# A hybrid decoder layer: the first norm's residual made in quarters beside the recurrence, and one branch chunk's seven products moved from the first block to the third

## The chip, the core and the metric

The kernel runs on one core of a Trainium2 chip. It is one launch that computes one decoder layer for 256 tokens in float32. The metric is the time on the device in microseconds, the lower the better. A core has engines that each run their own queue of instructions in order: TensorE (PE; PEld is its weight load) for matrix products, VectorE (DVE) and ScalarE (ACT) for elementwise work, GpSimd (POOL) and SyncE (SP), which in this kernel mostly issue DMA transfers. Engines wait for each other through semaphores.

## The reference

What matters of it here: a first SwiGLU with a residual and a norm gives `h`; from `h` come attention, a gated recurrence and gates; both branches are merged, and the residual of `h` is added again.

```python
h = layer_norm(DN_ALPHA * h + 0.5 * swiglu(h, ffn1_w_in[l], ffn1_w_out[l]), ln1_g[l], ln1_b[l])
q, k, v, qi, ki, wi, rx, rg, gates = split_cols(h @ w_in[l])
...
y_attn = dsa_attention(q, k, v, qi, ki, wi)
y_rnn = rglru_branch(rx, rg, conv_w[l], conv_b[l], lru_wa[l], lru_ba[l],
                     lru_wx[l], lru_bx[l], lru_lambda[l])
g_attn, g_rnn = jnp.split(jax.nn.sigmoid(gates), 2, axis=-1)
merged = g_attn * (y_attn @ w_attn_branch[l]) + g_rnn * (y_rnn @ w_rnn_branch[l])
h = layer_norm(DN_ALPHA * h + merged @ w_out[l], ln2_g[l], ln2_b[l])
h = layer_norm(DN_ALPHA * h + 0.5 * swiglu(h, ffn2_w_in[l], ffn2_w_out[l]), ln3_g[l], ln3_b[l])
```

The model width is 2048, the recurrence 2560 wide, and the layer norm ends with a product by `g` and a sum with `b`.

## The kernel before

**Weights.** Every weight matrix streams from HBM through SBUF once, in pieces of up to 128x1024 (class `Weights`). A piece is loaded by SP into a `raw` buffer (five of them), then split for exact products: ACT writes the high part `wh` (L245) and DVE the low part `wl` (L246), each with five buffers. The piece's number stands in the names that the lists of instructions below show: `wl585` is the low part of piece 585, loaded into `raw585`. SP can load piece n+5 only when DVE has split piece n. Some stretches of 4 x 128 rows (a chunk) are multiplied by seven products of half size in place of eight; such a chunk is loaded whole into an `rf` buffer (three of them), and DVE makes sums of its blocks first (`operand`, L208, L212, L215). `YR_FAST` says for each of the four 512-column blocks of the recurrent branch's product which of its five chunks are made that way; the others are plain.

**Order.** PE, SP and POOL run in the order in which the program is written. The order of DVE and ACT is set by a scheduler when the kernel is built, by its own estimate of when each operand is there; on the chip it is fixed. Work that is to run beside the products is written as generators; `Background.step` advances each by one `yield` whenever PE starts on a new piece.

**The recurrence** (the loop over `NR + LAG`) takes 80 pieces of `wB` and 24 of `lru`, pieces 570 to 673. Two pieces make one product of a 128-column block (`block3`, `wide3`: for each 128 rows L1437 with the high part, 512 columns, and L1438 with the low part, 256 columns). DVE then reduces the result (L1456, tile `t`), applies three taps of a convolution (L1476, tile `xg`) and splits it (L832, tile `xc`). After it come two gate blocks (pieces 674 to 689) and the recurrent branch's product (from piece 690), whose matrix products L716, L717 and L719 are those of `together`.

**The residual.** `h` after the first norm is needed again after the merge. Its normalized rows lie in DRAM in eight tiles `away[t][nb]` (two of 128 tokens, four of 512 columns; `ys37` to `ys44` in the lists), put there without gain and bias. While the recurrence runs, `residual_away` borrows the three `rf` buffers (tile `ry`): it loads the gain row for all partitions and the eight tiles, multiplies on DVE (L677), adds the bias with a DMA that accumulates in SBUF (L679), and stores the result to the same DRAM tiles (L681). All its DMAs are issued by POOL. `back` (L687) loads them later. A similar routine for the second norm, `residual`, adds its bias by L660; L1132 accumulates the feed-forward's partial results.

Of the kernel before, what the change touches and what calls it, by code (L numbers as in the profile page):

```python
# [12 lines left out]
OP = mybir.AluOpType  # L13
# [4 lines left out]
D = 2048  # L18
# [51 lines left out]
def block_plan(chunks, fills, lead=2, n=4, late=True):  # L70

    plain = [("c", k) for q in range(n) if q not in chunks for k in (4 * q, 4 * q + 2)]
    forms = [(f, q) for q in chunks for f in FORMS]
    rest = ["o"] * fills
    plan = [(rest.pop(), 0) for _ in range(min(lead, fills))] + plain[:1]
    plain = plain[1:]
    slow = []
    while plain or rest:  # L80
        for which in (plain, rest) if late else (rest, plain):
            if which:
                p = which.pop(0)
                slow.append((p, 0) if p == "o" else p)
    if not forms:
        return plan + slow
    step = len(forms) / (len(slow) + 1)
    n = 0
    for i, f in enumerate(forms):
        plan.append(f)  # L90
        while len(slow) > n and i + 1 >= (n + 1) * step:
            plan.append(slow[n])
            n += 1
    return plan
# [13 lines left out]
A_FAST = {b: () if b == 6 else ONE_A if b in (5, 1) else FAST_A for b in range(8)}  # L108
GATE_FAST = ((), (), (), (3,), FAST_A, FAST_A, (), ())
YA_FAST = ((), (0, 1), (0, 1), (0, 1))  # L110
YR_FAST = ((0, 1), (0, 1), (0,), (0,))
MG_FAST = ((), (0, 1), (0,))
YA_FORMS = (0, 1)
YR_FORMS = (0, 1)
# [207 lines left out]
def tile_layer(ctx, tc, x_fm, x_tm, pos, f1a, f1o, wA, wki, wB, wG, lru, wab, wrb, wo, f2a, f2o,  # L322
# [6 lines left out]
    V, A, T, G = nc.vector, nc.scalar, nc.tensor, nc.gpsimd  # L329
    count = [0]  # L330

    def name(s):
        count[0] += 1
        return f"{s}{count[0]}"

    def U(s="u", dt=F32):
        return pool.tile([P, 512], dt, name=name(s), tag="u", bufs=U_BUFS)
# [4 lines left out]
    def T1(s="t"):  # L342
        return temps.tile([P, S], F32, name=name(s), tag="t", bufs=T_BUFS)
# [22 lines left out]
    def block_pieces(ap, plan, fills=None, fo=None):  # L366
        chunk = {}
        for f, k in plan:
            if f == "c":
                pieces.append((ap[:, k * 512:k * 512 + PIECE], None))  # L370
            elif f == "o":
                g, nb, k = next(fills)
                k += 2 * SEGS[g][0]
                pieces.append((fo[nb][:, k * 512:k * 512 + PIECE], None))
            else:
                if k not in chunk:
                    chunk[k] = ap[:, k * 2048:(k + 1) * 2048]
                pieces.append((chunk[k], f))
# [28 lines left out]
    for i in range(NR + LAG):  # L407
        if i < NR:
            plain([wB[RX + i], wB[RG + i]])
        if i >= LAG:  # L410
            g, c = divmod(i - LAG, TPG)
# [5 lines left out]
    for b in range(4):  # L417
        block_pieces(wrb[b], block_plan(YR_FAST[b], 0, 0, NR // 4))
    for nb in range(3):
# [227 lines left out]
    def bias_row(b, nb, w=512):  # L647
        return bass.AP(tensor=b.tensor, offset=b.offset + nb * 512, ap=[[0, P], [1, w]])
# [13 lines left out]
    def residual_away(g, b):  # L662

        def wide():
            return W.fast_pool.tile([P, D], F32, name=name("ry"), tag="rf", bufs=RAWF_BUFS)

        gr, ys = wide(), [wide() for _ in range(2)]
        G.dma_start(gr, bias_row(g, 0, D))
        for t in range(2):
            for nb in range(4):  # L670
                G.dma_start(ys[t][:, nb * 512:(nb + 1) * 512], away[t][nb])
        for _ in range(8):
            yield
        for t in range(2):
            for o in range(0, D, 512):
                v = ys[t][:, o:o + 512]
                V.tensor_tensor(v, v, gr[:, o:o + 512], op=OP.mult)  # L677
                yield
            G.dma_start(ys[t], bias_row(b, 0, D), accum_op=OP.add)  # L679
            for nb in range(4):  # L680
                G.dma_start(away[t][nb], ys[t][:, nb * 512:(nb + 1) * 512])  # L681

    def back():
        for nb in range(4):
            for t in range(2):
                Y[t][nb] = U("y")
                G.dma_start(Y[t][nb], away[t][nb])  # L687
            yield
# [458 lines left out]
    away = [[spill.tile([P, 512], F32, name=name("ys")) for _ in range(4)] for _ in range(2)]  # L1147
# [12 lines left out]
    qT, kT, v, qiT = [None] * 8, [None] * 2, [None] * 2, [None] * 4  # L1160
# [186 lines left out]
    def token_tiles():  # L1347
        return [[spill.tile([P, 512], F32, name=name("gd")) for _ in range(2)] for _ in range(4)]

    ga, gr = token_tiles(), token_tiles()  # L1350
# [3 lines left out]
    def product(x, forms, fast):  # L1354

        c, e = blockF(x, forms, block_plan(fast, 0, 0, len(x) // 4), None)
        return (joined(c, e), True) if e else (c, False)
# [9 lines left out]
    def fetch(src):  # L1367
        r = []
        for t in range(2):
            u = U("gf")  # L1370
            G.dma_start(u, src[t])
            r.append(u)
        return r
# [11 lines left out]
    for nb in range(4):  # L1385
        g, got = got, fetch(ga[nb + 1]) if nb < 3 else None
        s, _ = product(ya, ya_forms, YA_FAST[nb])
# [62 lines left out]
    def block3(x):  # L1450
# [6 lines left out]
        return t  # L1457

    bg.add("away", residual_away(ln1_g, ln1_b))
    xgs, xcs, tiles = {}, {}, []  # L1460

# [6 lines left out]
    for j in range(NR + LAG):  # L1468
# [14 lines left out]
        if j >= LAG:  # L1483
            i = j - LAG
            g, c = divmod(i, TPG)
# [7 lines left out]
            vw, t = U("vw"), T1()  # L1493
# [3 lines left out]
            if c == TPG - 1:  # L1497
# [6 lines left out]
                vw, t, u = U("vw"), T1(), T1()  # L1504
                for n in range(2):
                    a, b = slice(64 * n, 64 * n + 64), slice(64 - 64 * n, 128 - 64 * n)
# [34 lines left out]
    for nb in range(4):  # L1541
        if nb == 3:
            bg.add("main", back())
        s, _ = product(yr, yr_forms, YR_FAST[nb])
        g, a = got
# [18 lines left out]
def _layout(x, positions, ffn1_w_in, ffn1_w_out, ln1_g, ln1_b, w_in, conv_w, conv_b, lru_wa, lru_ba,  # L1564
# [4 lines left out]
    def c(a):  # L1569
        return np.ascontiguousarray(a)  # L1570
# [12 lines left out]
    def f_in(w, plans):  # L1583
        fast = [sorted({k for f, k in plan if f in FORMS}) for plan in plans]
        return paired(w.reshape(NK, P, 2, NBK, 256).transpose(3, 1, 0, 2, 4).reshape(NBK, P, NK, 512), fast)

    def f_out(w):
        return paired(w.reshape(NKF, P, 4, 512).transpose(2, 1, 0, 3), [()] * 4)

    def a_blocks(w, fast):  # L1590
        n = w.shape[1] // 512
        nk = w.shape[0] // P
        return paired(w.reshape(nk, P, n, 512).transpose(2, 1, 0, 3), fast)
# [13 lines left out]
    def recurrent(wa, wx):  # L1607
        lr = np.zeros((GRP, P, 16, P), wa.dtype)
        for g in range(GRP):
            for c in range(GRP):  # L1610
                a, x = wa[g * GRP + c], wx[g * GRP + c]
                row = slice(32 * c, 32 * c + 32)
                x_col = slice(32 * (c ^ 2), 32 * (c ^ 2) + 32)
                half = 10 + 3 * (c // 2)
                for n, m, col in ((0, a, row), (1, x, x_col)):
                    lr[g, row, n] = m[P:, :P]
                    lr[g, :, 2 * c + 2 + n] = m[:P, :P]
                    lr[g, :, half + c % 2, col] = m[:P, P:]
                    lr[g, row, half + 2, col] = m[P:, P:]
        return lr.reshape(GRP, P, -1)  # L1620
# [4 lines left out]
    def pr(vec):  # L1625
# [11 lines left out]
        lru=recurrent(lru_wa[0], lru_wx[0]), wab=a_blocks(w_attn_branch[0], YA_FAST),  # L1637
        wrb=a_blocks(w_rnn_branch[0][order], YR_FAST),
        wo=a_blocks(w_out[0], MG_FAST + ((),)), f2a=f_in(ffn2_w_in[0], PLANS2), f2o=f_out(ffn2_w_out[0]), cols_d=c(cols),
# [18 lines left out]
```

## Time and profile before

| | |
|---|---|
| Time, median of 3 runs | 2234.37 us (2232.87 to 2234.55) |
| The profiled execution: its time | 2234.3 us |
| The profiled execution: its span | 2232.5 us |
| ACT busy | 1423.6 us (64%) |
| Moved from HBM | 468.83 MB read, 12.58 MB written |
| Chain that ended last, by engine | PE 66%, issue 26%, DVE 3%, DMA 2%, POOL 2% |

The span runs from the first instruction to the last; the time has 1.8 us around it. In the rows of the profile, a group is a line of the program on one engine, with the tiles it writes and reads; "x8 | 5.4, 687" means eight instructions, 5.4 us in total, 687 ns each on average; what follows names the idle time of the engine just before them and what ended it. In a timeline each row begins with the start and the duration in microseconds. In a row of waits stand who waited, for whom, the sum, the number of waits and the longest. In a row of stretches of time (`1366.70:1392.30`) stand the length, then the busy time of PE, PEld, DVE, ACT and POOL, the granted PE clock as a share of full speed, the DMA engines' busy share and their GB/s. "DMA to landing" is the time from the issue of a transfer to its completion (least, median, greatest).

### The profile page before, as it was taken

Reading aid. Unit: us, or ns where it says so; the run is one execution under the profiler, and the core shown is the slowest. Engines: PE = TensorE matmul, PEld = TensorE weight load, DVE = VectorE, ACT = ScalarE, POOL = GpSimd, SP = SyncE. Lnnn points to the kernel's source line nnn. Section 1 sums busy time; section 2 is a strip of 40 time slices with the busy share of each in tenths; the row PEclk is TensorE's granted clock in tenths of the full one; section 3 lists DMA queues with packets and bytes.
Section 4 is the critical chain, followed back from the end, with each engine's and each line's share of the span. In section 5 each row is a group of like instructions: output and inputs, shape, how many; then the busy total and the mean of one; then the engine's idle time right before and its main releaser. Section 6 shows DMA issues by size and latency. Waiting matters only on the chain.

```text
span 2232.5 us, 37406 instructions
## 1 busy us (share of the span) xinstructions
PE 2218.2 (99%) x13942; PEld 2034.9 (91%) x13942; DVE 2113.9 (95%) x3076; ACT 1423.6 (64%) x1967; POOL 136.2 (6%) x210
## 2 busy tenths in 40 slices
PE   9999999999999999999999999999999999999998
PEld 8999999999998898899989988998899999999997
DVE  8999999999999999799979889999999999999997
ACT  6666666666656655665567786555666666666663
POOL 0000000000001000001100001100100000000001
PEclk9999999999999999999999999999999999999999
DMA  9776766666675555648686658765877667676655
GB/s 341 235 227 227 237 214 224 237 221 235 228 238 200 185 197 174 208 141 309 231 280 200 192 186 311 253 216 190 260 235 230 237 219 243 219 245 216 218 200 189
DMA packets 128086, 504.83 MB, mean 226 GB/s; under 512 B 14848, under 2 KB 17664, under 8 KB 108832
## 3 DMA queue, kind: packets, MB, share of 16 engines
q1 hardware_dynamic: 107424, 451.98, 57.8%
q0 software_dynamic: 20480, 50.46, 9.6%
q8 instruction: 109, 1.79, 0.3%
q14 instruction: 73, 0.60, 0.1%
HBM read 468.83 MB, written 12.58 MB: 216 GB/s over the span
## 4 chain that ended last, share of the span: by engine, by line
PE 66%; issue 26%; DVE 3%; DMA 2%; POOL 2%; ACT 1%; SPq 0%; DVEq 0%; POOLq 0%; ACTq 0%
PE mm L716 14%; PE mm L719 13%; PE mm L717 13%; PE mm L1437 6%; PE bp L719 4%; PE bp L717 4%; PE bp L716 4%; PE mm L1438 3%; POOL y L1132 1%; DVE wl L246 1%; PE mm L704 1%; PE mm L702 1%; PE mm L703 1%; ACT wh L245 1%; DMA rf<-f2a 0%
## 5 line engine op out<-in xcount | busy, mean ns | idle before, releaser
L245 ACT ACTIVATE wh<-raw 128x1024 fp32r<-128x1024 f32 (+1 forms) x569 | 572.5, 1026 | 264.0 <-PE mm L717 174.4
L246 DVE TENSOR_TENSOR wl<-raw,wh 128x1024 fp32r<-128x1024 f32 (+1 forms) x569 | 661.3, 1182 | 55.8 <-ACT wh L245 55.0
L245 ACT ACTIVATE wh<-rf 128x1024 fp32r<-128x1024 f32 (+1 forms) x438 | 393.3, 914 | 191.8 <-PE mm L717 105.2
L246 DVE TENSOR_TENSOR wl<-rf,wh 128x1024 fp32r<-128x1024 f32 (+1 forms) x438 | 450.5, 1041 | 6.6 <-PE mm L719 1.2
L716 PE MATMUL mm<-wh,hs 128*128 128x512 f32 (+1 forms) x872 | 297.3, 350 | 0.0
L717 PE MATMUL mm<-wh,hs 128*128 128x512 f32 (+1 forms) x872 | 292.1, 344 | 0.0
L716 PE MATMUL mm<-wh,g 128*128 128x512 f32 x656 | 249.3, 380 | 0.0
L717 PE MATMUL mm<-wh,g 128*128 128x512 f32 x656 | 248.6, 379 | 0.0
L245 ACT ACTIVATE wh<-ws 128x1024 fp32r<-128x1024 f32 x146 | 155.4, 1064 | 120.5 <-PE mm L717 72.2
L716 PE MATMUL bp<-wh,sh 128*128 128x256 f32 x876 | 213.6, 278 | 0.0
L1437 PE MATMUL mm<-hs,wh 128*128 128x512 f32 x640 | 211.4, 383 | 1.1 <-ACT wh L245 1.1
L717 PE MATMUL bp<-wh,sl 128*128 128x256 f32 x876 | 210.7, 275 | 0.0
L719 PE MATMUL mm<-wl,hs 128*128 128x512 f32 (+1 forms) x872 | 205.1, 344 | 0.0
L208 DVE TENSOR_TENSOR ws<-rf 128x1024 f32<-128x1024 f32 x146 | 178.2, 1220 | 11.0 <-DMA rf<-f2a 3.9
L246 DVE TENSOR_TENSOR wl<-ws,wh 128x1024 fp32r<-128x1024 f32 x146 | 177.9, 1218 | 3.9 <-ACT wh L245 3.7
L716 PEld LDWEIGHTS mm<-wh,hs 128*128 128x128 f32 x872 | 165.8, 190 | 15.3 <-issue 1.3
L717 PEld LDWEIGHTS mm<-wh,hs 128*128 128x128 f32 x872 | 165.9, 190 | 13.6
L1438 PE MATMUL mm<-hs,wl 128*128 128x256 f32 x640 | 175.0, 273 | 1.7 <-DVE wl L246 1.7
L717 PEld LDWEIGHTS bp<-wh,sl 128*128 128x128 f32 x876 | 168.1, 192 | 1.2
L716 PEld LDWEIGHTS bp<-wh,sh 128*128 128x128 f32 x876 | 168.0, 192 | 1.2
L719 PE MATMUL mm<-wl,g 128*128 128x512 f32 x656 | 168.3, 379 | 0.0
L719 PEld LDWEIGHTS mm<-wl,hs 128*128 128x128 f32 x872 | 153.8, 190 | 15.5
(374 smaller groups left out, 4616.9 us busy)
## 6 DMA issues: line engine op xcount, KB each, us to landing
rf<-f1a SPq DMA_DIRECT2D x57, 1024.0 KB, 6.1
rf<-f2a SPq DMA_DIRECT2D x57, 1024.0 KB, 6.2
raw<-f1o SPq DMA_DIRECT2D x88, 512.0 KB, 7.8
raw<-f2o SPq DMA_DIRECT2D x88, 512.0 KB, 7.8
raw<-wB SPq DMA_DIRECT2D x80, 512.0 KB, 4.5
raw<-f2a SPq DMA_DIRECT2D x62, 512.0 KB, 3.9
raw<-f1a SPq DMA_DIRECT2D x61, 512.0 KB, 3.8
raw<-wG SPq DMA_DIRECT2D x54, 512.0 KB, 3.8
```

What stands on the lines that cost most here:

```text
L208: v.tensor_tensor(t, b[:, 0:4:3], b[:, 1:2].to_broadcast([P, 2, 4, P]), op=OP.add)
L245: self.last_h = nc.scalar.activation(hp, src, AF.Copy)
L246: self.last = nc.vector.tensor_tensor(lp, src, hp, op=OP.subtract)
L702: T.matmul(ps, xh, w[0], start=start, stop=False)
L703: T.matmul(ps, xh, w[1], start=False, stop=False)
L704: T.matmul(ps, xl, w[0], start=False, stop=stop)
L716: T.matmul(ps, xh, w[0], start=start, stop=False)
L717: T.matmul(ps, xl, w[0], start=False, stop=False)
L719: T.matmul(ps, xh, w[1], start=False, stop=stop)
L1132: G.dma_start(Y[t][nb], u, accum_op=OP.add)
L1437: T.matmul(ps.rearrange("p (a q h) -> p a q h", a=2, h=2), w[0], both, start=first, stop=False)
L1438: T.matmul(ps[:, :S].rearrange("p (q h) -> p q h", h=2), w[1], pairs(x[:, 0]), start=False, stop=last)
```

## The change

```diff
-YR_FAST = ((0, 1), (0, 1), (0,), (0,))
+YR_FAST = ((0,), (0, 1), (0, 1), (0,))
...
         gr, ys = wide(), [wide() for _ in range(2)]
-        G.dma_start(gr, bias_row(g, 0, D))
-        for t in range(2):
-            for nb in range(4):
-                G.dma_start(ys[t][:, nb * 512:(nb + 1) * 512], away[t][nb])
-        for _ in range(8):
-            yield
-        for t in range(2):
-            for o in range(0, D, 512):
-                v = ys[t][:, o:o + 512]
-                V.tensor_tensor(v, v, gr[:, o:o + 512], op=OP.mult)
+        for nb in range(4):
+            part = [v[:, nb * 512:(nb + 1) * 512] for v in (gr, *ys)]
+            G.dma_start(part[0], bias_row(g, nb, 512))
+            yield
+            for t in range(2):
+                G.dma_start(part[1 + t], away[t][nb])
                 yield
-            G.dma_start(ys[t], bias_row(b, 0, D), accum_op=OP.add)
-            for nb in range(4):
-                G.dma_start(away[t][nb], ys[t][:, nb * 512:(nb + 1) * 512])
+            for _ in range(5):
+                yield
+            for t in range(2):
+                V.tensor_tensor(part[1 + t], part[1 + t], part[0], op=OP.mult)
+                yield
+                G.dma_start(part[1 + t], bias_row(b, nb), accum_op=OP.add)
+            for _ in range(8):
+                yield
+            for t in range(2):
+                G.dma_start(away[t][nb], part[1 + t])
+                yield
```

The residual is made in four quarters of 512 columns, one after the other, each with its own gain load, two loads of y, two products, two accumulations and two stores, all of 256 KB; before, the gain and each accumulation were 1 MB, and the loads came first, then the products, then accumulations and stores. The bytes are the same. The number of DMAs goes from 19 to 28. In the branch, the second chunk is made by seven products in the blocks 2 and 3, no longer in 1 and 2, and the host lays out the weights accordingly. Lines after the change stand four lower than before (L246 is still L246; L1456 becomes L1460).

POOL's queue at the residual, before: from the last load to the first store of the second half (`ry787` and `ry788` are the two y tiles, `ry786` the gain, `ln1_b` the bias).

```order
L671 DMA ry788_12086<-ys44_235 128x512
L679 DMA ry787_12085<-ln1_b 128x2048
L681 DMA ys37_228<-ry787_12085 128x512
L681 DMA ys38_229<-ry787_12085 128x512
L681 DMA ys39_230<-ry787_12085 128x512
L681 DMA ys40_231<-ry787_12085 128x512
L679 DMA ry788_12086<-ln1_b 128x2048
L681 DMA ys41_232<-ry788_12086 128x512
```

POOL's queue now, from the start of the first quarter to the loads of the second:

```order
L670 DMA ry786_12084<-ln1_g 128x512
L673 DMA ry787_12085<-ys37_228 128x512
L673 DMA ry788_12086<-ys41_232 128x512
L680 DMA ry787_12085<-ln1_b 128x512
L680 DMA ry788_12086<-ln1_b 128x512
L684 DMA ys37_228<-ry787_12085 128x512
L684 DMA ys41_232<-ry788_12086 128x512
L670 DMA ry786_12084<-ln1_g 128x512
L673 DMA ry787_12085<-ys38_229 128x512
L673 DMA ry788_12086<-ys42_233 128x512
```

The loads of a quarter now stand behind the stores of the quarter before it, and a store reads what the accumulation has written. No other DMA of POOL stands between the quarters: the next one in its queue belongs to the gate blocks after the recurrence.

DVE's queue in the recurrence, before, at the splits of pieces 582 to 585 (`wl`), with the last two residual products in it:

```order
L246 TENSOR_TENSOR wl582_12299<-raw582_12145,wh582_12298 128x256
L677 TENSOR_TENSOR ry788_12086<-ry788_12086,ry786_12084 128x512 x2
L246 TENSOR_TENSOR wl583_12322<-raw583_12167,wh583_12321 128x1024
L1456 TENSOR_REDUCE t801_12342<-mm800_12295 128x256
L246 TENSOR_TENSOR wl584_12356<-raw584_12193,wh584_12355 128x1024
L1476 SCALAR_TENSOR_TENSOR xg802_12344<-t801_12342,cols_120,xg802_12344 128x255
L1476 SCALAR_TENSOR_TENSOR xg802_12344<-t801_12342,cols_120,xg802_12344 128x254
L1476 SCALAR_TENSOR_TENSOR xg802_12344<-t801_12342,cols_120,xg802_12344 128x253
L246 TENSOR_TENSOR wl585_12379<-raw585_12215,wh585_12378 128x1024
```

DVE's queue now at the same place. `ry788` in it is the second product of the second quarter, `ry787` the first product of the third:

```order
L246 TENSOR_TENSOR wl582_12293<-raw582_12138,wh582_12292 128x256
L678 TENSOR_TENSOR ry788_12086<-ry788_12086,ry786_12084 128x512
L246 TENSOR_TENSOR wl583_12316<-raw583_12161,wh583_12315 128x1024
L1460 TENSOR_REDUCE t801_12337<-mm800_12289 128x256
L246 TENSOR_TENSOR wl584_12351<-raw584_12187,wh584_12350 128x1024
L1480 SCALAR_TENSOR_TENSOR xg802_12339<-t801_12337,cols_120,xg802_12339 128x255
L1480 SCALAR_TENSOR_TENSOR xg802_12339<-t801_12337,cols_120,xg802_12339 128x254
L1480 SCALAR_TENSOR_TENSOR xg802_12339<-t801_12337,cols_120,xg802_12339 128x253
L678 TENSOR_TENSOR ry787_12085<-ry787_12085,ry786_12084 128x512
L836 TENSOR_TENSOR xc803_12344<-xg802_12339,xc803_12344 128x256
L246 TENSOR_TENSOR wl585_12374<-raw585_12209,wh585_12373 128x1024
L678 TENSOR_TENSOR ry788_12086<-ry788_12086,ry786_12084 128x512
```

Before, all eight products are behind DVE at split 583. Now the third quarter's products stand on both sides of split 585. The first quarter's stand on both sides of split 578, the second's around a reduction and split 582, and the fourth's here, between splits 588 and 589:

```order
L246 TENSOR_TENSOR wl588_12456<-raw588_12290,wh588_12455 128x1024
L678 TENSOR_TENSOR ry787_12085<-ry787_12085,ry786_12084 128x512
L1460 TENSOR_REDUCE t811_12475<-mm810_12430 128x256
L678 TENSOR_TENSOR ry788_12086<-ry788_12086,ry786_12084 128x512
L246 TENSOR_TENSOR wl589_12489<-raw589_12313,wh589_12488 128x1024
L1480 SCALAR_TENSOR_TENSOR xg812_12477<-t811_12475,cols_120,xg812_12477 128x255
```

SP's queue at the start of the recurrent branch, before, with the whole-chunk loads `rf691` and `rf698`, and now, with `rf691` alone in the first block and `rf703` as the second block's first:

```order
L181 DMA raw690_14988<-wrb 128x1024
L181 DMA rf691_15008<-wrb 128x2048
L181 DMA raw693_15059<-wrb 128x1024
L181 DMA raw695_15111<-wrb 128x1024
L181 DMA raw697_15162<-wrb 128x1024
L181 DMA rf698_15194<-wrb 128x2048
```

```order
L181 DMA raw690_14997<-wrb 128x1024
L181 DMA rf691_15017<-wrb 128x2048
L181 DMA raw692_15046<-wrb 128x1024
L181 DMA raw693_15070<-wrb 128x1024
L181 DMA raw695_15122<-wrb 128x1024
L181 DMA raw696_15151<-wrb 128x1024
L181 DMA raw698_15205<-wrb 128x1024
L181 DMA raw699_15229<-wrb 128x1024
L181 DMA raw701_15303<-wrb 128x1024
L181 DMA raw702_15321<-wrb 128x1024
L181 DMA rf703_15339<-wrb 128x2048
```

The first block's second whole-chunk load has become two plain ones; the second block begins with piece 702 in place of 704.

## The prediction

> **What bounds the kernel now.** I read the page first, then the waits and busy times of the stage that the change touches (1095 to 1150 us, the start of the recurrence), then its timelines engine by engine, and last the times that single DMAs took to land.
>
> ```profile
> span 2232.5 us, 37406 instructions
> PE 2218.2 (99%) x13942; PEld 2034.9 (91%) x13942; DVE 2113.9 (95%) x3076; ACT 1423.6 (64%) x1967; POOL 136.2 (6%) x210
> ```
>
> TensorE (PE) is busy for 99% of the span, so a change that leaves its products alone can only win back the few places where PE waits, or make new ones. VectorE (DVE) has 95%: it has hardly any slack to hide a wait of its own. What PE waits for between 1095 and 1400 us:
>
> ```profile
> PE mm L1438 <- DVE wl L246: 1.7, 3, 0.8
> PE mm L1437 <- ACT wh L245: 1.1, 1, 1.1
> PE bp L1427 <- ACT xc L831: 0.6, 1, 0.6
> PE mm L719 <- DVE wl L246: 0.4, 1, 0.4
> PE bp L1428 <- DVE xc L832: 0.3, 1, 0.3
> ```
>
> That is the whole pool: 4.1 us. Two of these rows belong to the residual. PE's timeline (start, duration) shows the place, and the two times at which PE reaches pieces 585 and 589, which the sum below needs (each full piece of weights is eight pairs of L1437 and L1438; counting them along PE's order gives the piece):
>
> ```profile
> 1125.01 0.38 PE L1437 MATMUL mm<-hs,wh 128*128 128x512 f32 x1
> ...
> 1133.76 0.27 PE L1438 MATMUL mm<-hs,wl 128*128 128x256 f32 x1
> ...
> 1136.05 0.27 PE L1438 MATMUL mm<-hs,wl 128*128 128x256 f32 x1
> 1137.41 0.48 PE L1437 MATMUL mm<-hs,wh 128*128 128x512 f32 x1 [1.09 <-ACT wh L245]
> 1138.67 0.38 PE L1438 MATMUL mm<-hs,wl 128*128 128x256 f32 x1 [0.78 <-DVE wl L246]
> ```
>
> Undisturbed, a pair starts 0.33 us after the one before it (0.22 + 0.11). From 1136.05 to 1138.67 there are 2.62 us for 0.33, so this stall costs **2.3 us** from start to start. The row for L719 above, **0.4 us**, is the one that the moved chunk bears on: it lies in the branch's first block, at 1377 us. Why the stall at 1136 is there is in these DMA rows (issues at 1124.5 us, and the same load from 1150 to 1300 us):
>
> ```profile
> ry<-ln_b POOLq DMA_DIRECT2D x1, 1024.0 KB, 13.0
> raw<-wB SPq DMA_DIRECT2D x1, 512.0 KB, 11.7
> ...
> raw<-wB SPq DMA_DIRECT2D x51, 512.0 KB, 4.3
> ```
>
> Piece 590 was loaded beside the residual's 1 MB accumulation and took 11.7 us, against 4.3 us later. DVE's own queue shows the second half of the story:
>
> ```profile
> 1100.27 1.21 DVE L246 TENSOR_TENSOR wl<-raw,wh 128x1024 fp32r<-128x1024 f32 x1
> 1101.40 0.42 DVE L832 TENSOR_TENSOR xc<-xg,xc 128x256 fp32r<-128x256 f32 x1
> 1106.53 0.69 DVE L677 TENSOR_TENSOR ry<-ry,ry 128x512 f32<-128x512 f32 x1 [4.71 <-DMA ry<-ys]
> ...
> 1109.07 1.22 DVE L246 TENSOR_TENSOR wl<-raw,wh 128x1024 fp32r<-128x1024 f32 x1
> 1110.20 0.68 DVE L677 TENSOR_TENSOR ry<-ry,ry 128x512 f32<-128x512 f32 x1
> ...
> 1116.40 0.68 DVE L1456 TENSOR_REDUCE t<-mm 128x256 f32<-128x512 f32 x1
> 1117.00 0.42 DVE L246 TENSOR_TENSOR wl<-raw,wh 128x256 fp32r<-128x256 f32 x1
> 1117.33 1.29 DVE L677 TENSOR_TENSOR ry<-ry,ry 128x512 f32<-128x512 f32 x2
> ```
>
> A residual product whose data has not landed stops DVE for 4.71 us, with the split of piece 579 standing behind it. DVE runs its queue in order, so **every split behind a residual product waits for that product's DMA**. This is what the forecast rests on.
>
> **The change: what goes.** The 1 MB transfers go; the bytes stay. I count the 2.3 us at 1136 as gone: the load of piece 590 no longer shares the DMA engines with 1 MB transfers, and by the sum below PE comes to it late anyway. The 0.4 us at 1377 goes too: a seven-product chunk in place of a plain one costs DVE one sum of 128x1024 (as long as a full split above, 1.2 us), two of 128x512 (as a residual product, 0.7 each) and splits of 1024 and 512 columns more (1.9), together 4.5 us, and these leave the first block, where PE waited 0.4 us. PE's own work is the same, since one chunk changes places with a plain one.
>
> In the third block the 4.5 us come back:
>
> ```profile
> 1366.70:1392.30 25.60, 25.19 (x157) 22.90 (x156) 25.43 (x36) 17.45 (x24) 7.52 (x14) 1.00 0.80 302
> 1418.00:1444.40 26.40, 26.40 (x150) 23.78 (x149) 25.40 (x40) 14.41 (x19) 3.62 (x7) 1.00 0.78 269
> ```
>
> These are the first and the third block (length; then PE, PEld, DVE busy). DVE has 1.0 us free in the third, so up to 3.5 us could show; but the lead that DVE gains in the first block carries on through the second, and the cover is the same work done earlier. I take nothing, with 3.5 us as the other end.
>
> **What is added: a chain of three round trips.** The order of POOL shows that nothing there waits for the pieces of weights: the new `yield`s only place instructions within the queue. Each quarter of the residual needs the quarter before it accumulated and stored, since POOL's queue is in order too. And DVE's order holds the products at fixed places: beside splits 578, 582, 585 and 589. So the question is whether the DMAs of a quarter finish in the time that DVE needs from one place to the next. The time C from the end of a quarter's second product to the start of the next quarter's first is made of POOL's steps:
>
> ```profile
> 1096.30 3.19 POOL L671 DMA_DIRECT2D ry<-ys  x6 [0.16 <-issue]
> ...
> 1111.19 0.89 POOL L679 DMA_DIRECT2D ry<-ln_b  x1 [5.43 <-DVE ry L677]
> 1122.18 2.17 POOL L681 DMA_DIRECT2D ys<-ry  x4 [10.11 <-DMA ry<-ln_b]
> ```
>
> An issue is 0.53 us (3.19 / 6). From the product's end (1110.20 + 0.68) to the accumulation's issue are 0.3 us. That accumulation landed after 10.5 us, at 1121.7, and the store followed 0.5 us later; I take 0.4. Then come one store and the gain's load (0.53 each) before the load of y is issued, and 0.1 us to wake DVE: 1.9 us in all. To this come an accumulation of 256 KB and a load of 256 KB. The trace has neither at this place, but the same sizes elsewhere:
>
> ```profile
> L660 POOL DMA_DIRECT2D y<-ln_b x8: 848/866/1206, 1575.1 to 1602.3; - x8
> DMA to landing us min/median/max: 5.3/7.7/12.3
> L1132 POOL DMA_DIRECT2D y<-yd x80: 852/918/1241, 71.1 to 2177.7; - x80
> DMA to landing us min/median/max: 3.3/6.1/12.1
> L687 POOL DMA_DIRECT2D y<-ys x8: 538/538/538, 1406.5 to 1426.4; - x8
> DMA to landing us min/median/max: 2.8/4.7/6.0
> ```
>
> L660 is the very accumulation (a bias row, 256 KB). I take its least, 5.3 us, because a stopped DVE frees no raw buffers and so slows the loads of weights beside it; for the load the median of L687, 4.7 us. **C = 5.3 + 4.7 + 1.9 = 11.9 us.** The ends are 3.3 + 2.8 + 1.9 = 8.0 and 12.3 + 6.0 + 1.9 = 20.2.
>
> **The sum.** By DVE's steps in a row (from start to start a product 0.6, a reduction 0.6, xc 0.35, a full split 1.13, a short one 0.35):
> - First quarter: y for the first product is issued at about 1096.3 and lands 4.7 later, at 1101.0; product, xc, split 578, product end at **1104**. Before, this was 1106.5 for the first product alone: a gain of some 5 us.
> - Second quarter at 1104 + C = 1115.9. Without a wait DVE would be there at about 1110 (split 579, reduction, split 580, three taps, split 581, xc: 5.6 us). Product, reduction, split 582, product: 2.15 us, to 1118.05.
> - Third quarter at 1118.05 + C = 1129.95; product, xc, split 585 done 2.1 later, at 1132. PE reached 585 at 1125.0: **about 7 us of stall**. With the second product 2.7 us, to 1132.65.
> - Fourth at 1132.65 + C = 1144.55; product, reduction, product, split 589: 2.95, to **1147.5**. PE needed it at 1133.8.
>
> So PE is 13.7 us late at piece 589; written out, 3C − 22.0. From there on PE and DVE go on as before, with DVE's lead near nothing, as it was at 590 already. The time is 2234.3 (the profiled execution; the median of the three runs, 2234.37, is the same to 0.1) − 2.3 − 0.4 + 13.7 = **2245.3 us**, 0.5% slower.
>
> [...]
>
> **The rivals.**
> - *The round trips are short.* Up to C = 9.7 us the loss (7.1) less the 2.7 us won stays within 0.2%, about what a measurement of this kernel can tell from no change. With the least of both kinds of row, C = 8.0, the loss is 2.0 and the time **2233.6**. For it: while DVE stands, the DMA engines are less busy. Against it: the least of eight bias accumulations is 5.3, and the load stands behind a store and the gain's load. Chance 0.18. [...]
> - *The residual is really spread, and no product waits* (the mechanism that the loop suggests; it decides where C falls under 7.3 us). The time is 2234.3 − 2.7 = **2231.6**, and only if the DVE time won also removed the other waits of the list (0.9 at L1438, 0.9 at L1427 and L1428) would it be 2229.8, which is just faster by over 0.2%. DVE's order, with all eight products within twelve pieces, speaks against it. Chance of that 0.03.
> - *The DMA engines stay full*, as in the windows around L660, whose accumulations took up to 12.3: with the medians, 7.7 + 4.7 + 1.9, C is 14.3, the loss 20.9 and the time 2252.5. This is the upper end of the forecast, not another case.
> - *The third block pays* up to 3.5 us: 2248.8, chance 0.1 within the forecast.
>
> **How the numbers follow.** The forecast (slower, by C over 9.7) has 0.79, no measurable change 0.18, faster 0.03. The range goes from C = 8.7 (loss 4.1: 2235.7) to a little over C = 14.3: **2235.5 to 2253**. Outside stay the least of both rows at once, and accumulations of 12.3 in a row.
>
> **What would show it.** In the profile after: three waits of DVE at the residual product, of some 6 to 9 us each, put down to the DMA of ry; POOL waiting for ry from ln_b between them; PE idle at L1437 or L1438 in two places 10 to 15 us apart, put down to the splits, with some 14 us in all; nothing left at 590 and in the branch's first block. I am wrong if DVE's products find their data there, or if a quarter's round trip takes under 9 us. I am wrong in the last step if PE makes up the delay later, which at 99% busy it can't.

## The result, and the profile after

| | before | after |
|---|---|---|
| time, median of 4 runs (lowest to highest) | 2234.46 us (2232.87 to 2234.62) | 2262.02 us (2261.32 to 2262.48) |
| ratio, 95% interval | | 1.0125 [1.0107, 1.0142] |
| profiled execution: time, span | 2234.3, 2232.5 us | 2261.32, 2259.5 us |

The change makes the kernel 1.25% slower. The prediction named the direction and the place; its 2245.3 us and its upper end of 2253 are too low. The head of the page after:

```profile
span 2259.5 us, 37417 instructions
PE 2228.8 (99%) x13942; PEld 2042.6 (90%) x13942; DVE 2113.0 (94%) x3076; ACT 1422.9 (63%) x1967; POOL 143.1 (6%) x219
```

The same numbers of instructions on PE and DVE, the same busy time of DVE: so the 27 us are not more work but waits, and matmuls that took longer (PE's 10.6 us more; see the clock below). DVE's waits from 1090 to 1165 us (total, times, longest):

```profile
DVE ry L678 <- DMA ry<-ys: 29.8, 4, 10.5
```

and what PE waits for from 1090 to 1480 us, in place of the 4.1 us of before:

```profile
PE mm L1442 <- DVE wl L246: 12.6, 5, 6.3
PE bp L1452 <- DVE wl L246: 3.0, 1, 3.0
PE mm L723 <- DVE wl L246: 2.0, 2, 1.4
PE bp L723 <- DVE wl L246: 0.8, 1, 0.8
```

DVE stops for 29.8 us at four residual products, and PE runs dry behind the splits that stand after them. DVE's timeline at the products (start, duration, and in brackets the idle time before and what ended it):

```profile
1104.67 0.69 DVE L678 TENSOR_TENSOR ry<-ry,ry 128x512 f32<-128x512 f32 x1 [3.42 <-DMA ry<-ys]
...
1106.75 0.68 DVE L678 TENSOR_TENSOR ry<-ry,ry 128x512 f32<-128x512 f32 x1
...
1121.62 0.69 DVE L678 TENSOR_TENSOR ry<-ry,ry 128x512 f32<-128x512 f32 x1 [8.42 <-DMA ry<-ys]
...
1123.16 0.69 DVE L678 TENSOR_TENSOR ry<-ry,ry 128x512 f32<-128x512 f32 x1
...
1136.25 0.69 DVE L678 TENSOR_TENSOR ry<-ry,ry 128x512 f32<-128x512 f32 x1 [7.52 <-DMA ry<-ys]
...
1138.33 0.69 DVE L678 TENSOR_TENSOR ry<-ry,ry 128x512 f32<-128x512 f32 x1
...
1153.04 0.69 DVE L678 TENSOR_TENSOR ry<-ry,ry 128x512 f32<-128x512 f32 x1 [10.46 <-DMA ry<-ys]
```

From the end of a quarter's second product to the start of the next quarter's first are 14.2 us (1106.75 + 0.68 to 1121.62), 12.4 and 14.0: the round trip C, 13.5 in the mean. POOL's timeline shows what it is made of:

```profile
1097.19 1.11 POOL L673 DMA_DIRECT2D ry<-ys  x2 [0.16 <-issue]
...
1107.73 0.87 POOL L680 DMA_DIRECT2D ry<-ln_b  x1 [1.18 <-DVE ry L678]
...
1115.31 0.56 POOL L684 DMA_DIRECT2D ys<-ry  x1 [3.99 <-issue]
1115.87 0.55 POOL L670 DMA_DIRECT2D ry<-ln_g  x1
1116.41 1.07 POOL L673 DMA_DIRECT2D ry<-ys  x2
...
1124.40 0.88 POOL L680 DMA_DIRECT2D ry<-ln_b  x1 [0.89 <-DVE ry L678]
...
1130.19 0.56 POOL L684 DMA_DIRECT2D ys<-ry  x1 [2.27 <-DMA ry<-ln_b]
...
1131.28 1.07 POOL L673 DMA_DIRECT2D ry<-ys  x2
...
1139.32 0.87 POOL L680 DMA_DIRECT2D ry<-ln_b  x1 [1.18 <-DVE ry L678]
...
1146.29 0.56 POOL L684 DMA_DIRECT2D ys<-ry  x1 [3.79 <-DMA ry<-ln_b]
...
1147.38 1.08 POOL L673 DMA_DIRECT2D ry<-ys  x2
```

From the second accumulation's issue to its store are 7.6, 5.8 and 7.0 us (the DMA view puts its landing at 7.0, 5.2 and 6.7); from the issue of the next loads to DVE's product are 5.2, 5.0 and 5.7. PE's timeline around its second and third stall:

```profile
1132.89 0.38 PE L1441 MATMUL mm<-hs,wh 128*128 128x512 f32 x1
1138.47 0.58 PE L1442 MATMUL mm<-hs,wl 128*128 128x256 f32 x1 [5.20 <-DVE wl L246]
```

```profile
1149.42 0.38 PE L1441 MATMUL mm<-hs,wh 128*128 128x512 f32 x1
1156.13 0.58 PE L1442 MATMUL mm<-hs,wl 128*128 128x256 f32 x1 [6.32 <-DVE wl L246]
1156.50 0.63 PE L1441 MATMUL mm<-hs,wh 128*128 128x512 f32 x1
1156.92 0.42 PE L1442 MATMUL mm<-hs,wl 128*128 128x256 f32 x1
1157.14 0.64 PE L1441 MATMUL mm<-hs,wh 128*128 128x512 f32 x1
```

The matmul at 1156.13 is the first of piece 589 with its low half; before, it started at 1133.76. PE is 22.4 us late there; 0.9 of it is from earlier (y for the first quarter is issued at 1097.19, before at 1096.30). Behind the stall a pair starts 0.64 us after the one before it (1156.50 to 1157.14), not 0.33. The granted clock (in the windows below: length; busy time of PE, PEld, DVE, ACT, POOL; clock; DMA share; GB/s) says why; before, it was 1.00 up to 2230 us. After, then before:

```profile
1100.00:1115.00 15.00, 15.00 (x94) 13.79 (x93) 9.70 (x15) 6.40 (x9) 2.33 (x3) 1.00 0.81 214
1115.00:1130.00 15.00, 11.59 (x69) 9.55 (x68) 6.54 (x10) 5.04 (x7) 4.52 (x7) 0.77 0.74 231
1130.00:1145.00 15.00, 9.80 (x44) 8.49 (x43) 6.06 (x8) 2.81 (x5) 4.49 (x7) 0.77 0.73 191
1145.00:1160.00 15.00, 8.68 (x43) 7.61 (x43) 6.88 (x11) 3.30 (x6) 4.51 (x7) 0.80 0.73 213
```

```profile
1115.00:1130.00 15.00, 15.00 (x110) 13.38 (x109) 14.28 (x21) 9.35 (x14) 3.07 (x5) 1.00 1.00 296
1130.00:1145.00 15.00, 13.13 (x82) 11.70 (x82) 8.16 (x13) 6.85 (x11) 2.15 (x4) 1.00 0.99 311
```

Last, the branch. DVE stops there at the first sum of the second block's first seven-product chunk (`rf703` in SP's queue above), and SP's queue shows when that chunk's raw columns (`rf`) were asked for:

```profile
1408.53 1.23 DVE L208 TENSOR_TENSOR ws<-rf 128x1024 f32<-128x1024 f32 x1 [6.92 <-DMA rf<-wrb]
```

```profile
1374.20 23.69 SPq L181 DMA_DIRECT2D raw<-wrb  x8
1398.06 0.33 SPq L181 DMA_DIRECT2D rf<-wrb  x1
```

The load stands behind eight plain loads, each of which needs a raw buffer that a split sets free, and is issued at 1398.06; DVE is at its sum at 1401.6 and stands for 6.9 us, with the splits of the first block's last pieces behind it. So the load that comes late is not that of the moved chunk, which now lies in the third block, but the one that is next in the queue since the first block's second whole-chunk load is gone.

Where the 27.0 us are, counted along PE's order as the time from each matmul's start to the next one's beyond its own pitch at full clock:

| stretch | before | after | difference |
|---|---|---|---|
| up to 30 us | 3.8 | 5.0 | +1.2 |
| 30 to 1090 us | 18.6 | 18.6 | 0.0 |
| recurrence with the residual (1090 to 1165; after, to 1192) | 3.0 | 24.1 | **+21.1** |
| rest of the recurrence | 4.1 | 3.8 | -0.3 |
| the branch's first three blocks | 1.0 | 3.8 | **+2.8** |
| the rest | 5.3 | 7.5 | +2.2 |

### The profile page after: what moved, and what is told of

It is laid out like the page before. It is cut to its first block, busy times and chain, and to the rows that moved or that the text cites. A ratio compares the mean times of both kernels' runs of the same rounds, so it can differ in the third digit from the quotient of the medians.

```text
span 2259.5 us, 37417 instructions
## 1 busy us (share of the span) xinstructions
PE 2228.8 (99%) x13942; PEld 2042.6 (90%) x13942; DVE 2113.0 (94%) x3076; ACT 1422.9 (63%) x1967; POOL 143.1 (6%) x219
## 4 chain that ended last, share of the span: by engine, by line
PE 61%; issue 27%; DMA 4%; DVE 4%; POOL 2%; ACT 1%; SPq 0%; DVEq 0%; POOLq 0%; ACTq 0%
PE mm L720 13%; PE mm L723 13%; PE mm L721 13%; PE mm L1441 4%; PE bp L723 3%; PE bp L721 3%; PE bp L720 3%; PE mm L1442 2%; DVE wl L246 2%; POOL y L1136 1%; DMA rf<-wrb 1%; ACT wh L245 1%; DMA ry<-ys 1%; DMA ry<-ln_b 1%; PE mm L708 1%
## 5 line engine op out<-in xcount | busy, mean ns | idle before, releaser
L246 DVE TENSOR_TENSOR wl<-raw,wh 128x1024 fp32r<-128x1024 f32 (+1 forms) x569 | 663.0, 1185 | 49.3 <-ACT wh L245 48.5
L246 DVE TENSOR_TENSOR wl<-rf,wh 128x1024 fp32r<-128x1024 f32 (+1 forms) x438 | 452.1, 1045 | 5.3 <-PE mm L723 0.6
L1441 PE MATMUL mm<-hs,wh 128*128 128x512 f32 x640 | 217.9, 391 | 0.0
L246 DVE TENSOR_TENSOR wl<-ws,wh 128x1024 fp32r<-128x1024 f32 x146 | 178.6, 1223 | 3.7 <-ACT wh L245 3.6
L721 PEld LDWEIGHTS mm<-wh,hs 128*128 128x128 f32 x872 | 166.1, 190 | 13.5
```

The lines of the kernel that those rows point to most:

```text
L246: self.last = nc.vector.tensor_tensor(lp, src, hp, op=OP.subtract)
L721: T.matmul(ps, xl, w[0], start=False, stop=False)
L1441: T.matmul(ps.rearrange("p (a q h) -> p a q h", a=2, h=2), w[0], both, start=first, stop=False)
```

## The experiments

Each ratio is to the kernel before on the same chip, whose medians lay between 2234.24 and 2234.59 us. Where nothing else is said, a kernel with the quarters has the seven-product chunks at their old places (the `YR_FAST` line of the first diff below). In the diffs, `...` stands for lines left out.

**Which half of the change costs.** The first kernel has the quarters and the old places of the seven-product chunks, the second the old residual and the moved chunk.

Quarters alone, against the changed kernel:

```diff
-YR_FAST = ((0,), (0, 1), (0, 1), (0,))
+YR_FAST = ((0, 1), (0, 1), (0,), (0,))
```

Chunk alone, against the kernel before:

```diff
-YR_FAST = ((0, 1), (0, 1), (0,), (0,))
+YR_FAST = ((0,), (0, 1), (0, 1), (0,))
```

> The quarters as in the change, the branch's chunks as before. Theory: the recurrence loses what it lost in the changed kernel (24.0 us of PE stalls between 1100 and 1200 us against 3.5 before), and the branch's stalls are back at 0.9 us, so the time is 2262.0 - 2.9 = about 2259 us. Rival: the branch's stalls of 3.8 us come from the late residual and not from the moved chunk; then it stays at about 2262.

> The branch's chunk moved as in the change, the residual as before. Theory: DVE stands at the sum of the second block's first whole chunk until its late load lands, as in the changed kernel (6.9 us), and PE loses some 3 us in the branch's first two blocks: 2234.4 + 2.9 = about 2237.3 us. Rival (the step of the prediction): the move takes 4.5 us of DVE work out of the first block and wins 0.4 us: 2234.0.

Quarters alone: 2257.24 us (2256.56 to 2259.86), ratio 1.0103 [1.0088, 1.0118]. Chunk alone: 2236.63 us (2235.31 to 2237.86), ratio 1.001 [1.0, 1.0019], an interval that reaches down to no change. The quarters make some 23 us, the chunk some 2 alone and 4.8 on top of the quarters. The branch in the trace of the chunk alone (DVE's waits from 1360 to 1440 us):

```profile
DVE ws L208 <- DMA rf<-wrb: 7.6, 1, 7.6
```

The same wait as in the change, so it comes from the chunk, not from the quarters before it.

**Is it the order of the loads?** If the loss is three serial round trips, it must go when the order of POOL's queue is changed: here all twelve loads stand ahead of the first accumulation, while products, accumulations and stores stay in quarters.

```diff
+        parts = [[v[:, nb * 512:(nb + 1) * 512] for v in (gr, *ys)] for nb in range(4)]
         for nb in range(4):
-            part = [v[:, nb * 512:(nb + 1) * 512] for v in (gr, *ys)]
-            G.dma_start(part[0], bias_row(g, nb, 512))
-            yield
+            G.dma_start(parts[nb][0], bias_row(g, nb, 512))
             for t in range(2):
-                G.dma_start(part[1 + t], away[t][nb])
-                yield
-            for _ in range(5):
+                G.dma_start(parts[nb][1 + t], away[t][nb])
+        for nb in range(4):
+            part = parts[nb]
+            for _ in range(8):
                 yield
```

> Quarters, with all twelve loads issued ahead of the first accumulation, the branch as before. The transfers have the same sizes and number as in the change; only the round trip between quarters is gone. Theory: DVE waits at the first products alone, by at most the 5.3 us of before, and the time is 2231 to 2236 us. Rival: it is the many transfers of 256 KB themselves that cost; then the time stays above 2245.

2232.48 us (2231.85 to 2233.56), ratio 0.9989 [0.9979, 0.9998]. The whole loss of the quarters is gone, with the same 28 DMAs of the same sizes. The scheduler set the products closer together here than in the change (all eight stand ahead of split 583 again), so it is not their places that took the loss away. DVE's waits at the products:

```profile
DVE ry L678 <- DMA ry<-ys: 4.6, 2, 3.9
```

The next kernel leaves POOL's queue as the change has it and holds DVE's products back instead, each behind the split that is the newest where the program writes it (582, 602, 622 and 642 for the first of each quarter).

```diff
             for t in range(2):
-                V.tensor_tensor(part[1 + t], part[1 + t], part[0], op=OP.mult)
+                with tc.issue_after(W.last.ins):
+                    V.tensor_tensor(part[1 + t], part[1 + t], part[0], op=OP.mult)
                 yield
```

> Quarters and POOL's queue exactly as in the change, the branch as before; each product is held behind the split that was made last when it was written, so that the products stand 20 pieces apart (behind splits 582, 602, 622 and 642). Theory: each quarter has some 60 us for its round trip of 13.5, DVE never waits at a product, and the time is 2231 to 2236 us. Rival: the chain of DMAs itself or its traffic slows the weights; then over 2245.

2234.78 us (2232.63 to 2235.36), ratio 1.0 [0.9991, 1.001]. The three round trips are all still there, and no product waits, since DVE comes to them 20 pieces apart. So neither the small DMAs nor the round trips cost anything by themselves; they cost because the products stand in DVE's in-order queue a few splits apart. It is no gain either: PE stands once near the end of the recurrence, at a place where it stood 0.6 us before the change too. The last products run some 50 us earlier (at 1252.8 and 1255.1), and that they cause it is not shown.

```profile
1305.34 0.38 PE L1443 MATMUL mm<-hs,wl 128*128 128x256 f32 x1 [1.42 <-DVE wl L246]
```

**Does the loss follow the length of the trip?** Now the next quarter's loads are issued right behind a quarter's accumulations, and its stores only after them.

```diff
-        for nb in range(4):
+        for nb in range(5):
+            if nb < 4:
...
+                for t in range(2):
+                    G.dma_start(part[1 + t], away[t][nb])
...
+            for t in range(2):
+                if nb:
+                    G.dma_start(away[t][nb - 1], done[1 + t])
...
```

> The residual in quarters, the branch's chunk as before the change; GpSimd's queue issues a quarter's gain and loads right behind the accumulations of the quarter before, and the stores of that quarter only after them, so that a round trip no longer holds the wait for the accumulation's landing (5.8 to 7.6 us in the changed kernel's trace). Theory (the loss is the length of the serial round trip, three times): a trip is 0.3 + 1.4 + 5.2 + 0.1 = 7.0 us, later ones about 8, instead of 13.5; split 585 is then done some 7 to 8 us after TensorE needs it, so 2238 to 2243 us, TensorE's stalls of the recurrence 7 to 9 us in sum, DVE's waits at the products 3 of 3 to 6 us. Rival (each quarter's boundary has its price whatever it waits for, by more and smaller DMAs): as the quarters alone, 2255 or more, and stalls of 15 us.

2256.24 us (2254.23 to 2256.66), ratio 1.0096 [1.0082, 1.011]: a miss, and by the number the rival's. Its trace holds two reasons. The times of the DMAs from issue to landing between 1094 and 1160 us (count, size, median) are, in this kernel

```profile
ry<-ys POOLq DMA_DIRECT2D x8, 256.0 KB, 9.2
ry<-ln_b POOLq DMA_DIRECT2D x8, 256.0 KB, 5.8
```

and in the change

```profile
ry<-ys POOLq DMA_DIRECT2D x8, 256.0 KB, 5.4
ry<-ln_b POOLq DMA_DIRECT2D x8, 256.0 KB, 5.0
```

A load issued beside the accumulations takes 9.2 us, not 5.4, so the trip fell only from 13.5 to 11.0. And the products moved: the scheduler set the second quarter's ahead of split 581, the third's ahead of 583 and the fourth's around 585, where the change has 582, 585 and 589. With fewer splits between the quarters, DVE waited 7.7, 8.0 and 6.9 us at them, and PE's delay fell on a piece that it needs earlier. Two things had been changed at once. The next kernel keeps the queue of this one and holds the products at the places of the change.

```diff
+                self.made[self.split] = self.last.ins
...
-                V.tensor_tensor(part[1 + t], part[1 + t], part[0], op=OP.mult)
+                with tc.issue_after(W.made[((577, 578), (581, 582), (584, 585), (588, 588))[nb][t]]):
+                    V.tensor_tensor(part[1 + t], part[1 + t], part[0], op=OP.mult)
```

> As the run with the stores behind the next quarter's loads, but with the eight products held at the splits where the change has them (beside 578, 582, 585 and 589), so that only the length of the round trip differs from the quarters alone. Theory (three round trips, counted from the places of the products): with trips of 11.0 us, as that run had, instead of 13.5 (quarters alone: 13.9, 13.0 and 13.5), the delay at piece 589 is 7.4 us less: 2257.2 - 7.4 = 2249.8 us, within 2247 to 2252; VectorE waits 5 to 8 us at the first product of each quarter. Rival (the length of the trip does not set the loss; the wait of 8 us at a product is the price of each quarter, wherever it stands and whatever GpSimd waits for): 2255 to 2258 us, as with the quarters alone and as with the stores late.

2248.08 us (2246.68 to 2249.44), ratio 1.0061 [1.0044, 1.0078]: within the theory's interval and outside the rival's. DVE at the last product of each quarter and the first of the next:

```profile
1107.32 0.69 DVE L689 TENSOR_TENSOR ry<-ry,ry 128x512 f32<-128x512 f32 x1
1118.73 0.69 DVE L689 TENSOR_TENSOR ry<-ry,ry 128x512 f32<-128x512 f32 x1 [4.95 <-DMA ry<-ys]
1120.28 0.69 DVE L689 TENSOR_TENSOR ry<-ry,ry 128x512 f32<-128x512 f32 x1
1132.54 0.69 DVE L689 TENSOR_TENSOR ry<-ry,ry 128x512 f32<-128x512 f32 x1 [7.73 <-DMA ry<-ys]
1135.54 0.69 DVE L689 TENSOR_TENSOR ry<-ry,ry 128x512 f32<-128x512 f32 x1
1145.51 0.69 DVE L689 TENSOR_TENSOR ry<-ry,ry 128x512 f32<-128x512 f32 x1 [5.72 <-DMA ry<-ys]
```

The trips are 10.7, 11.6 and 9.3 us, 8.8 less in all than with the quarters alone (13.9, 13.0 and 13.5), and the time is 9.2 less. So what sets the loss is the length of the trip against the splits that stand between two quarters; the run with the stores late is explained by the places of its products.

The number of trips was varied too: two halves of 1024 columns, with one trip between them.

```diff
-        for nb in range(4):
-            part = [v[:, nb * 512:(nb + 1) * 512] for v in (gr, *ys)]
-            G.dma_start(part[0], bias_row(g, nb, 512))
+        for h in range(2):
+            part = [v[:, h * 1024:(h + 1) * 1024] for v in (gr, *ys)]
+            G.dma_start(part[0], bias_row(g, 2 * h, 1024))
...
```

> The residual in two halves of 1024 columns, each of which waits for the half before it as the quarters do; the branch's chunk as before the change. Theory (a price per serial round trip): one trip instead of three, of about 17 us (an accumulation of 512 KB, stores, a gain and the loads), against some 11 us of DVE's work between the halves; one wait of DVE at a product, of 5 to 8 us, one stall of TensorE of 4 to 7, and 2238 to 2242 us. Rival (what costs is that the loads are issued late, however few trips there are): 2250 or more.

2244.54 us (2243.16 to 2245.62), ratio 1.0043 [1.0028, 1.0058]: far under the rival and 2.5 us over the theory's interval. There is one long wait, after a trip of 19.4 us (the second product of the first half starts at 1108.88 and takes 1.23) where 17 had been expected:

```profile
1129.48 1.22 DVE L679 TENSOR_TENSOR ry<-ry,ry 128x1024 f32<-128x1024 f32 x1 [10.35 <-DMA ry<-ys]
```

**What the moved chunk costs.** Two kernels issue the late load of the branch ahead of the eight plain loads that it stood behind, one with the old residual, one with the quarters. The expectations call it the moved chunk's load; by SP's queue it is that of the second block's first seven-product chunk, `rf703`.

```diff
+    W.prefetch(1)
     gate_block(7)
```

> The old residual and the moved chunk, with the chunk's raw load for the third block's place ahead of the eight raw loads that it stood behind. Theory (the moved chunk's loss is the late load, before which VectorE stops 7 to 8 us): no wait of VectorE at the sum of that chunk over 2 us, no stall of TensorE over 1.5 us in the branch's first two blocks, and 2233 to 2234.5 us, against 2236.6 of the moved chunk alone. Rival (the third block has no room for 4.5 us more of VectorE's work): 2236 or more, with TensorE's waits now in the third block.

> The whole change, with the raw load of the moved chunk's two pieces issued ahead of the eight raw loads that it stands behind in the queue of the weights' loads. Theory (what the moved chunk costs within the change is the late load): the 2.9 us of TensorE's stalls at 1400 to 1460 us go, VectorE's wait of 6.9 us at the chunk's first sum falls under 2 us, and the time is that of the quarters alone or up to 2 us above it: 2257 to 2259 us. Rival (within the change the chunk costs by VectorE's work in the third block, 4.5 us, since the quarters have taken the lead that would hide it): 2261 or more, with TensorE's stalls now at 1440 to 1480 us.

With the old residual: 2234.28 us (2232.27 to 2235.9), ratio 0.9999 [0.999, 1.0008]. With the quarters: 2257.32 us (2256.15 to 2258.61), ratio 1.0101 [1.0084, 1.0117], which is the time of the quarters alone. In the second kernel's trace the sum that had waited 6.92 us runs without a wait,

```profile
1402.38 1.23 DVE L208 TENSOR_TENSOR ws<-rf 128x1024 f32<-128x1024 f32 x1
```

PE's excess in the branch's first three blocks falls from 3.8 to 0.3 us, and no stall turns up in the third block in its place. So by the times the late load is the whole price, and the third block takes the 4.5 us of DVE's work without a stall. Of the 4.7 us by which the change gets faster, the branch in the trace accounts for 3.5; where the rest lies is not shown.

**Both repairs together:** the loads first, as in the diff above, and the moved chunk with the branch's late load early; against the changed kernel it has also

```diff
+    W.prefetch(1)
     gate_block(7)
```

> The change's quarters with all twelve loads ahead of the first accumulation, and the moved chunk with its raw load early. If both losses are what the theories say (late loads in GpSimd's queue, a late raw load in the branch), nothing waits at either place: 2231.5 to 2233 us, no wait of VectorE over 5 us at the products or at the chunk's sum. Rival (the two parts want the same raw buffers and DMA time): 2234.5 or more.

2232.4 us (2231.22 to 2233.15), ratio 0.9989 [0.998, 0.9998], the same as the loads first without the moved chunk. What it is ahead of the kernel before is 0.1%, at the edge of what the comparison can tell.

## Why the prediction's path was right and its time was not

The measured 2262.0 us lies above the range of 2235.5 to 2253. The path was right: the products wait, and PE runs dry behind them. Four steps of the sum failed: the length of a round trip C, the first quarter's load, PE's pace after a stall (a term that was missing), and the 0.4 us that the branch was to win.

Right, and shown by experiment: the direction; that the products wait in DVE's in-order queue and the splits behind them starve PE; that POOL's queue makes three serial trips (they stopped costing when the loads went ahead of them, or the products further apart); that PE doesn't make up the delay; that the third block takes the moved work for nothing. Of the signs named, the three waits at the product were there (8.4, 7.5 and 10.5 us for some 6 to 9), put down to the DMA of ry. PE stood 14.6 us in all, for some 14, but in three places and not two (3.0, 5.2 and 6.3 us): the sum had no stall behind the second quarter. The branch's first block was not free of stalls.

The sum was too small. It had 13.7 - 2.3 - 0.4 = 11.0 us, and the span grew by 27.0.

- **C = 11.9 us.** Measured 13.5, and 3C makes it **+4.9**. The accumulation that a trip waits for, the second of its quarter, landed after 6.3 in the mean where I had taken the least of eight, 5.3, with the argument that a standing DVE slows the loads beside it. Up to the store it took 6.8, against 5.3 and 0.4. The load took 5.3 with DVE's wake, against 4.7 and 0.1. POOL's other steps were 1.4, as taken. In the windows of the trips the DMA engines were 0.73 to 0.74 busy, less than the 0.99 to 1.00 of before, so the argument's premise held, and these accumulations were not at their least all the same. The first of each quarter's two landed after 4.1 to 4.8; that they slow each other is not shown.
- **The first quarter, done at 1104.** It was done at 1107.4, which is 1106.5 less the 0.9 us by which this execution ran later: **+2.5**. The loads of y, issued at 1097.19, let the first product start at 1104.67, after 7.5 us against the 4.7 taken; they are issued while the weights' loads still run (the DMA engines are 0.92 to 0.93 busy from 1097 to 1105 us). With both measured values the formula of the prediction gives 1106.5 + 40.6 + 7.8 - 1133.8 = 21.1 us of delay at piece 589, and the trace has 22.4 - 0.9 = 21.5. Up to there the sum was well built, and two of its terms too small.
- **"From there on PE and DVE go on as before."** PE went on at half clock for 4.6 us (from 1156.13 until about 1160.7, when the pairs come down to 0.33 again), and lost some **2.3**: six pairs of 0.64 for 0.33 are 1.9, and the half pairs at both ends 0.4. This term was missing. It is counted from the trace; no kernel here has such a stall without the half clock (behind it the 5 us windows show 0.54 with the quarters alone, 0.50 with the stores late, the halves and the change with the early load). The first two stalls have it as well, but there DVE is late again before PE has used up what lies ready, so it should cost nothing of its own. The prediction forecast a stall of 7 us and had no row that shows PE after such a stall.
- **"The 0.4 us at 1377 goes."** PE's excess in these blocks grew by **2.8** instead. What failed is the step "these leave the first block": only DVE's work was counted, not where the next whole-chunk load then stands in SP's queue (the second block's `rf703`, issued at 1398.06 behind eight plain loads) and not that its first sum stands in DVE's queue ahead of the first block's last splits. Both could have been read from the order of the program.
- **"2.3 us at 1136 go."** They went (there is no stall at piece 590 after), but it is a soft number: with the old residual and the early load of the chunk, the same place cost 1.0 us in that execution.

The recurrence: +21.1 measured, 13.7 - 2.3 = 11.4 forecast, and 4.9 + 2.5 + 2.3 is the difference of 9.7. The branch: 2.8 + 0.4 = 3.2. The other 3.1 us lie before the change's place and behind it (1.2 up to 30 us, 2.2 in the rest, -0.3 in between). In the other ten kernels' traces the first of these is 3.8 to 4.6 us and the rest 6.4 to 7.8, also in those that are as fast as before; so I take most of it for scatter between executions; what moves it stays open.

Why the range missed: its upper end took C = 14.3 and nothing else. The first quarter's load, the branch and PE's pace after a stall had no upper bound of their own in it, and all three came out dearer.

## What to carry to other kernels

Here a transfer cut into pieces cost nothing by its pieces (2232.48 us with all 28 DMAs, the loads first) and a lot by its order (2257.24 us with the quarters alone). If piece n+1's load stands behind piece n's store in one in-order queue, each boundary is a full round trip (here 12 to 14 us with pieces of 256 KB), and an in-order engine that consumes the pieces hands that wait to the work queued behind it (here 26.4 us of DVE's waits behind the three trips, and 14.6 us in which PE stood). So issue the loads ahead (it cost one reordering, and took the 23 us back), or set the consumers further apart than a round trip (2234.78 us with the products held back). When a step is moved, look up where its loads, and the loads behind them, then fall in their own queue, and what stands behind the first instruction that waits.

## What was not expected of the hardware

- **TensorE's clock after a stall.** Times of stalls are here from the matmul before to the one after, beyond its pitch. Behind the first 30 us, the stalls of 2.15 us (the chunk alone) and of 3.3, 5.4 and 6.5 us (the change) were followed by half clock, as were those of 2.6 us and more in the other kernels between 1100 and 1166 us (granted 0.50 to 0.66 in a window behind each). Those of up to 1.6 us were not (1.57 in the branch of the change, 1.59 in the kernel with the products held back; the clock stayed at 1.00), nor the 2.3 us of before that came in two parts (idle 1.09 and 0.78), while 2.4 us in three parts (idle 0.66, 0.35 and 0.78), in the kernel with the products at the same places, were. So the length alone does not tell. In the kernel with the chunk alone, the stall of 2.15 us at 1385.2 was followed by this:

```profile
1388.00:1392.00 4.00, 4.00 (x19) 3.74 (x18) 4.00 (x5) 1.56 (x3) 0.00 (x0) 0.57 1.04 409
```

  There the drop began about 1 us after PE had started again and lasted 3.4 us. In the change it lasted until about 1143.7 after the stall that ended at 1138.47, and until 1160.7 after the one that ended at 1156.13. Away from the program's ends, the stretches of half clock in these windows last one, two or three times 3.41 us: 3.4 with the chunk alone, 6.83 each in the change (1123.21 to 1130.04, 1136.86 to 1143.69 and 1153.93 to 1160.76), 10.2 with the halves. So what a stall costs behind it also depends on where in such a stretch it ends (in the change 5.2 us of it were left at 1138.47, 4.6 at 1156.13).
- **Accumulating DMAs of 256 KB.** The second of a quarter's two took 5.8 to 7.6 us to its store, with DMA engines that were three quarters busy (0.73 to 0.74). A load that is put beside two of them took 9.2 us in place of 5.4, so taking the wait out of the queue saved 2.5 us of the 13.5 of a trip, not the some 6 that had been expected.
